# Sums of weight halves for the down product: from GpSimd subtracts during the up product to accumulating DRAM transfers, half of them in the front stages

## The chip, the cores and the metric

The kernel runs on one core of a Trainium2 chip (TensorE = PE, VectorE = DVE, ScalarE = ACT, GpSimd = POOL, and SyncE = SP, which here only issues DMAs). The metric is the device time of one execution, in microseconds (us); less is better. Times of three executions are given, and the trace of one of them.

## The reference

One layer of a bidirectional encoder block on 512 tokens of 1024 channels, all float32. What matters for the change is the last part, the channel mixer:

```python
h = rmsnorm(x, norm1_w); proj = h @ w_in          # p | q | k | v | z | gates | g_pool | g_dn
y_pool = (pooled p, linear map, scale) @ pool_out
o = gated_delta_rule(q, k, v) forward + backward   # 8 heads of 128, chunks of 64
y_dn = (rmsnorm(o) * silu(z)) @ dn_out
x = x + (sigmoid(g_pool) * y_pool + sigmoid(g_dn) * y_dn) @ w_o

h2 = rmsnorm(x, norm2_w)
u = dwconv_centered(h2 @ ffn_up, ffn_conv_w, ffn_conv_b)      # 1024 -> 2 * 2816, width 3
gate, val = split(u)
x = x + (silu(gate) * val) @ ffn_down                         # 2816 -> 1024
return rmsnorm(x, final_norm_w)
```

## The kernel before

**Products.** Each float32 operand is split into a rounded high part and a low part, and a product is three matmuls: high by high, high by low, low by high (`mm3`, L370). For the weights of a job, SP loads a block of 1024 x 128 (L387, 512 KB, `wr_...`), ACT casts it to the high part (L392, `wh_...`), and POOL subtracts the high part from the raw block in two halves (L396, `wl_...`). A matmul on the first half of the rows needs the first half of `wl`. The raw blocks live in a ring of three buffers, `wh` and `wl` in rings of two (`RINGS`, L243). A job of the up product is 24 matmuls of 512 columns.

**Stages.** First come the norm and the products with w_in (jobs named p, z, q, k, v, gp, gd), mixed with the pooled branch and the delta rule. The eight heads are taken in two groups of four. For each group the inverse of small triangular blocks is worked out on DVE (L897, L901), its rows are stored to DRAM scratch by SP (L923, `u_scr` and `e_scr`), and loaded again in another arrangement by `spread_unit` (L927): `nm` by SP, `ext` by ACT's queue (L944). `merge_unit` (L951) then begins with the matmuls `l1a` (L962), which read `nm` and `ext`. After that come dn_out, pool_out, w_o, the second norm, the up product (44 jobs, two for each of 22 blocks of 128 channels, followed by the convolution, SiLU and multiplication), the down product and the final norm.

**The down product** is done as seven products of half size in place of eight (`ORDER`, L1623: 1, 7, 5, 6, 3, 2, 4). The tokens are halved (`T_H`), the output columns are halved (`N_H`), and the 22 blocks of ffn_down's rows are two halves of `HK` = 11. Products 1, 2 and 3 take a quarter of ffn_down as their right operand; products 5, 6, 7 and 4 take the difference of two quarters. These differences are kept in DRAM, `t_scr[4, 11, 128, 512]`, index 0 for product 5, 1 for 6, 2 for 7 and 3 for 4. `right_operand` (L1820) says where a product reads, `down_weights` (L1830) loads two blocks of 128 x 512 at once (L1844, `wr_dn`), has ACT cast them (L1865) and POOL or DVE subtract (L1868). The left operands are combinations of the token halves, made by `combine` and `split_part` (L1634, L1641). When a product is complete, `done` (L1876) adds it to the residual `x2` by `dadd` (L1744).

**How the differences are made.** `t_unit` (L1649) is called for every second of the 22 channel blocks of the up product (L1714). It has SP load row block i of both halves of ffn_down into SBUF (L1656, two loads of 512 KB into `tp`), POOL do four subtracts (L1665), the third and fourth of which use the results of earlier ones, and SP store each difference of 256 KB to `t_scr` (L1667).

**What sets the order.** All steps are tasks with an engine, a cost, a key, buffers that they read and write, and for transfers a size. `Planner` (L38) schedules the list by these costs: an engine that is free takes the ready task with the lowest key, buffers of a ring are handed out in the order of the program, and a transfer is taken to occupy one shared channel at 280 KB per us and to land some us after its issue. The result is a fixed order per engine, and every engine works its own queue strictly in that order. A changed cost or task can so move instructions that have nothing to do with it. Keys begin with FEED (weights), EVICT (taking away results), CHAIN (delta rule) or a unit's number, in this order of rank. `after=` names buffers whose tasks must be done before a task may start.

Of the kernel before, what the change touches and what calls it, by code (L numbers as in the profile page):

```python
# [9 lines left out]
F32 = mybir.dt.float32  # L10
# [4 lines left out]
P = 128  # L15
# [180 lines left out]
def cp(n):  # L196
    return 0.17 + n * 0.0023
# [12 lines left out]
def hybrid_block(  # L210
# [1412 lines left out]
    ENDS = ((0, 1, 3), (0, 0, 2), (1, 1, 6), (1, 0, 4))  # L1623
    a_raw = [None, None]
# [24 lines left out]
    def t_unit(i, u):  # L1649

        b = {}

        def load(r):
            if "w" not in b:
                b["w"] = pools["fp"].tile([P, 2, D], F32, tag="tp", bufs=RINGS["tp"], name=f"tp_{i}")
            k = i + HK * r  # L1656
            sp.dma_start(b["w"][:, r, :], ffn_down[0][k * P : (k + 1) * P, :])

        w = lambda r, c: b["w"][:, r, N_H[c]]
        n = lambda r, c: f"tp:{i}#{r}{c}"  # L1660
        for r in range(2):
            L(512, lambda r=r: load(r), r=["pool:fp"], w=[n(r, 0), n(r, 1)], key=u)

        for j, o, x, y in ((0, (0, 0), (0, 1), (0, 0)), (2, (0, 1), (1, 1), (0, 1)), (1, (1, 1), (1, 1), (0, 0)), (3, (1, 0), (1, 0), (1, 1))):
            G(cp(512), lambda o=o, x=x, y=y: pool.tensor_tensor(out=w(*o), in0=w(*x), in1=w(*y), op=ALU.subtract),  # L1665
              r=[n(*x), n(*y)], w=[n(*o)], key=u)
            L(256, lambda j=j, o=o: sp.dma_start(t_scr[j, i], w(*o)), r=[n(*o)], w=[f"ts{j}#{i}"], key=u)  # L1667

    def conv3(box, pp, ci, b, j, u):
# [16 lines left out]
        for k in (0, 2):  # L1686
            V(0.78, lambda k=k: tap(k), r=[pp], w=[yn], key=EVICT + u)

    for c in range(NF):
# [20 lines left out]
        else:  # L1710
            i = c - HK
            combine(*blk(i, 1), blk(i, 1)[0], blk(c, 1)[0], [f"ar{c}#1"], ALU.add, u + 1)
            combine(*blk(i, 0), blk(i, 1)[0], blk(i, 0)[0], [f"ar{i}#1"], ALU.subtract, u + 2)
        if c % 2 == 0:  # L1714
            t_unit(c // 2, u + 60)
# [28 lines left out]
    def dadd(p, j, i, t, c0, c1):  # L1744
        dve.tensor_tensor(out=x2[t][:, c0:c1], in0=acc[accn(p, j, i)[1]][:, 0 : c1 - c0], in1=x2[t][:, c0:c1], op=ALU.add)
# [64 lines left out]
    def left_operand(p, key):  # L1810

        for i in range(0, HK, 2):
            n = min(2, HK - i)
            if p == 3:
                (x, xn), (y, yn) = blk(i + HK, 0, n), blk(i, 0, n)
                combine(y, yn, x, y, xn, ALU.subtract, key + 50 * i, n)
# [3 lines left out]
    def right_operand(p, k0, n):  # L1820
# [5 lines left out]
        return t_scr[j, k0 : k0 + n].rearrange("k p c -> p k c"), [f"ts{j}#{k}" for k in range(k0, k0 + n)]  # L1826
# [3 lines left out]
    def down_weights(p, kk, u):  # L1830
# [15 lines left out]
        L(n * 256, load, r=deps, w=[rn], key=FEED + u)  # L1846
# [119 lines left out]
```

## Time and profile before

| | |
|---|---|
| time, median of three executions | 892.42 us (890.75 to 892.56) |
| time of the profiled execution | 890.88 us |
| its span, first to last instruction | 889.2 us |
| PE busy | 874.7 us (98%) |
| POOL busy | 497.9 us (56%) |
| DVE busy, ACT busy | 549.0 us (62%), 461.0 us (52%) |
| granted PE clock, mean | 0.996 |
| DMA moved | 140.20 MB, mean 158 GB/s |
| HBM read, written | 114.08 MB, 25.20 MB |

In a row of the profile's groups stand line, engine, operation and tiles (output <- inputs, partitions x elements), a count, then busy us and mean ns of one, then the idle time of the engine ahead of these instructions and what ended most of it. A row of the list of waits gives the waiting instruction, what released it, us in all, count, and the longest. A row of the timeline gives start, duration, engine, line, operation, tiles and, in brackets, the idle time before. SPq and ACTq are the queues on which SP and ACT issue DMAs; the duration there is that of the issue. Rows of DMA issues end with the KB of one and the median us from issue to landing; rows of DMA queues hold packets, MB and the share of 16 engines' span. Matmuls overlap, so PE's starts tell more than its ends.

### The profile page before, as it was taken

What the parts mean: (1) busy time and instruction counts of PE and PEld (TensorE: products, weight loads), DVE (VectorE), ACT (ScalarE), POOL (GpSimd) and SP (SyncE); (2) the same over time, 40 slices, a digit from 0 to 9 for tenths busy, and PEclk for the clock granted to TensorE, in tenths of its full rate; (3) what the DMA queues carried; (4) which work ended last, traced back from release to release, by engine and by line L of the source; (5) the groups of instructions that cost most, each with busy time, mean ns of one, the idle gap of its engine ahead of it and who ended that gap; (6) DMA issues with size and microseconds to landing.
All of it is one profiled execution on the core that took longest, in us unless ns stands there. A gap on an engine that the chain in (4) does not pass through costs nothing.

```text
span 889.2 us, 14088 instructions
## 1 busy us (share of the span) xinstructions
PE 874.7 (98%) x5178; PEld 737.1 (83%) x5178; DVE 549.0 (62%) x980; ACT 461.0 (52%) x791; POOL 497.9 (56%) x447
## 2 busy tenths in 40 slices
PE   8999999999999999999999999999999999999996
PEld 7888888798878887988788888888888888888885
DVE  4757685357795976554434244656655554569995
ACT  6689533418868334335854334444443333456664
POOL 3444555125455553253668706778787764567663
PEclk9999999999999999999999999999999999999999
DMA  7365449324255376112898606567666753266553
GB/s 207 99 204 131 130 118 188 86 60 119 64 163 154 108 168 107 31 60 73 275 306 270 190 1 231 187 213 225 233 202 203 244 173 101 97 211 181 186 178 133
DMA packets 176265, 140.20 MB, mean 158 GB/s; under 512 B 32110, under 2 KB 143547, under 8 KB 176196
## 3 DMA queue, kind: packets, MB, share of 16 engines
q1 hardware_dynamic: 167300, 137.20, 51.1%
q10 hardware_dynamic: 8896, 2.10, 1.6%
q8 instruction: 41, 0.67, 0.3%
q14 instruction: 28, 0.23, 0.1%
HBM read 114.08 MB, written 25.20 MB: 157 GB/s over the span
## 4 chain that ended last, share of the span: by engine, by line
PE 92%; DVE 3%; ACT 2%; DMA 2%; issue 1%; SPq 0%; DVEq 0%; ACTq 0%
PE ps_up L372 9%; PE ps_up L371 9%; PE ps_up L373 9%; PE dn L373 3%; PE dn L371 3%; PE dn L372 3%; PE ps_k L371 2%; PE pw L1139 2%; PE o L1176 2%; PE ps_k L373 2%; PE ps_gp L371 2%; PE ps_k L372 2%; PE ps_wo L373 2%; PE ps_wo L372 2%; PE ps_wo L371 2%; PE ps_gp L372 2%
## 5 line engine op out<-in xcount | busy, mean ns | idle before, releaser
L396 POOL TENSOR_TENSOR wl_up<-wr_up,wh_up 128x512 fp32r<-128x512 f32 x88 | 115.2, 1330 | 50.1 <-ACT wh_up L392 47.9
L372 PE MATMUL ps_up<-h_lo,wh_up 128*128 128x512 f32 (+1 forms) x368 | 139.9, 380 | 0.3 <-DVE h_lo L541 0.3
L371 PE MATMUL ps_up<-h_hi,wh_up 128*128 128x512 f32 (+1 forms) x368 | 140.0, 380 | 0.0
L373 PE MATMUL ps_up<-h_hi,wl_up 128*128 128x512 f32 (+1 forms) x368 | 139.8, 380 | 0.0
L1680 DVE SCALAR_TENSOR_TENSOR c<-ps_up,fw,c 128x511 f32<-128x511 f32 x88 | 66.0, 750 | 99.3 <-ACT c L1674 97.5
L1665 POOL TENSOR_TENSOR tp<-tp 128x512 f32<-128x512 f32 x44 | 59.9, 1362 | 43.4 <-DMA tp<-in_ffn_down_dram 38.5
L1868 POOL TENSOR_TENSOR w_dn<-wr_dn,w_dn 128x512 fp32r<-128x512 f32 x44 | 65.6, 1504 | 29.0 <-ACT w_dn L1865 27.5
L372 PEld LDWEIGHTS ps_up<-h_lo,wh_up 128*128 128x128 f32 x368 | 69.1, 188 | 13.5 <-DVE h_lo L541 0.5
L371 PEld LDWEIGHTS ps_up<-h_hi,wh_up 128*128 128x128 f32 x368 | 69.1, 188 | 13.3
L373 PEld LDWEIGHTS ps_up<-h_hi,wl_up 128*128 128x128 f32 x368 | 69.1, 188 | 13.2
L392 ACT CAST wh_up<-wr_up 128x1024 fp32r<-128x1024 f32 x44 | 46.2, 1051 | 62.1 <-issue 22.3
L1865 ACT CAST w_dn<-wr_dn 128x512 fp32r<-128x512 f32 x69 | 42.4, 621 | 29.5 <-PE dn L373 21.1
L372 PE MATMUL dn<-w_dn,as 128*128 128x512 f32 x141 | 54.2, 385 | 0.0
L371 PE MATMUL dn<-w_dn,as 128*128 128x512 f32 x141 | 54.2, 384 | 0.0
L373 PE MATMUL dn<-w_dn,as 128*128 128x512 f32 x141 | 54.2, 384 | 0.0
L1634 DVE TENSOR_TENSOR as<-a,as 128x512 fp32r<-128x512 f32 (+1 forms) x41 | 41.8, 1044 | 0.1
L1630 ACT CAST as<-a 128x512 fp32r<-128x512 f32 (+1 forms) x41 | 21.5, 534 | 32.5 <-DVE a L1701 28.9
L396 POOL TENSOR_TENSOR wl_k<-wr_k,wh_k 128x512 fp32r<-128x512 f32 x16 | 20.3, 1288 | 31.6 <-ACT wh_k L392 22.4
L396 POOL TENSOR_TENSOR wl_v<-wr_v,wh_v 128x512 fp32r<-128x512 f32 x16 | 20.4, 1294 | 27.5 <-ACT wh_v L392 27.5
L1674 ACT ACTIVATE c<-ps_up,fw 128x512 f32<-128x512 f32 x44 | 33.9, 770 | 0.0
L396 POOL TENSOR_TENSOR wl_z<-wr_z,wh_z 128x512 fp32r<-128x512 f32 x16 | 20.3, 1292 | 23.5 <-ACT wh_z L392 19.9
L396 POOL TENSOR_TENSOR wl_gp<-wr_gp,wh_gp 128x512 fp32r<-128x512 f32 x16 | 21.5, 1360 | 19.6 <-ACT wh_gp L392 18.0
(361 smaller groups left out, 2435.8 us busy)
## 6 DMA issues: line engine op xcount, KB each, us to landing
wr_up<-in_ffn_up_dram SPq DMA_DIRECT2D x44, 512.0 KB, 3.9
tp<-in_ffn_down_dram SPq DMA_DIRECT2D x22, 512.0 KB, 5.3
t_scr<-tp SPq DMA_DIRECT2D x44, 256.0 KB, 2.5
wr_dn<-t_scr SPq DMA_DIRECT2D x20, 512.0 KB, 3.8
wr_dn<-in_ffn_down_dram SPq DMA_DIRECT2D x15, 512.0 KB, 3.6
x<-in_x_dram SPq DMA_DIRECT2D x8, 512.0 KB, 6.1
wr_k<-in_w_in_dram SPq DMA_DIRECT2D x8, 512.0 KB, 5.9
wr_z<-in_w_in_dram SPq DMA_DIRECT2D x8, 512.0 KB, 3.9
```

Source lines behind the costliest of these rows:

```text
L371: pe.matmul(ps, ahi, bhi, start=first, stop=False)
L372: pe.matmul(ps, ahi, blo, start=False, stop=False)
L373: pe.matmul(ps, alo, bhi, start=False, stop=last)
L392: act.copy(b["hi"], b["raw"])
L396: pool.tensor_tensor(out=b["lo"][:, sl], in0=b["raw"][:, sl], in1=f32(b["hi"][:, sl]), op=ALU.subtract)
L1630: act.copy(sets[p][:, i : i + n, 0, :], src())
L1634: dve.tensor_tensor(out=w[:, :, 1, :], in0=src(), in1=f32(w[:, :, 0, :]), op=ALU.subtract)
L1665: G(cp(512), lambda o=o, x=x, y=y: pool.tensor_tensor(out=w(*o), in0=w(*x), in1=w(*y), op=ALU.subtract), r=[n(*x), n(*y)], w=[n(*o)], key=u)
L1674: act.activation(b[j], box["ps"], AF.Identity, scale=fw[:, 1, ci : ci + 1], bias=fw[:, 3, ci : ci + 1])
L1680: dve.scalar_tensor_tensor(out=y[:, lo:hi], in0=box["ps"][:, lo + sh : hi + sh], scalar=fw[:, k, ci : ci + 1], in1=y[:, lo:hi], op0=ALU.mu ...
L1865: act.copy(b["w"][:, 0, :], raw["t"][:, j, :])
L1868: eng.tensor_tensor(out=b["w"][:, 1, :], in0=raw["t"][:, j, :], in1=f32(b["w"][:, 0, :]), op=ALU.subtract)
```

## The change

`t_unit` and its call are gone. In its place twelve calls of `right_sums`, each for one of the four scratch indices (in the order 0, 2, 1, 3) and four, four or three blocks of rows. Each call issues two DMAs on POOL's queue. The first copies a quarter's rows of ffn_down from DRAM to `t_scr` (for indices 1 and 3 it copies the sum that stands at index 0 or 1); the second adds another quarter's rows to that place in DRAM, by a transfer that accumulates. The planner is told 1.2 us of POOL's time for each and a landing after 12 us. Each first transfer is tied to the result of a job by its mark: six are front jobs (z3, z5, gd0, gd2, q4, q5), six are jobs of the up product (blocks 2, 5, 8, 11, 14, 17). So 24 transfers on POOL's queue take the place of 22 loads and 44 stores on SP's and 44 subtracts on POOL.

Sums take the place of differences. The signs are made good elsewhere: two combinations of the left operand change between add and subtract, and `dadd` adds or subtracts by the table `MINUS`, with `x2` as its first operand and PSUM as its second. The loads of right operands now also wait for the pool "fp" to be open, which the up product opens.

```diff
+    MINUS = ((0, 1, 1), (1, 1, 1), (1, 1, 7), (0, 1, 6), (1, 1, 6))
...
-    def t_unit(i, u):
...
-            L(512, lambda r=r: load(r), r=["pool:fp"], w=[n(r, 0), n(r, 1)], key=u)
...
-            G(cp(512), lambda o=o, x=x, y=y: pool.tensor_tensor(out=w(*o), in0=w(*x), in1=w(*y), op=ALU.subtract),
-              r=[n(*x), n(*y)], w=[n(*o)], key=u)
-            L(256, lambda j=j, o=o: sp.dma_start(t_scr[j, i], w(*o)), r=[n(*o)], w=[f"ts{j}#{i}"], key=u)
+    def right_sums(j, k0, n, key, after):
+
+        rows = lambda r: slice((k0 + HK * r) * P, (k0 + n + HK * r) * P)
+        block = lambda r, c: ffn_down[0][rows(r), N_H[c]]
+        flat_ = lambda j: t_scr[j, k0 : k0 + n].rearrange("k p c -> (k p) c")
+
+        first, second = {0: ((0, 0), (0, 1)), 1: (0, (1, 1)), 2: ((0, 1), (1, 1)), 3: (1, (1, 0))}[j]
+        kept = isinstance(first, int)
+        name = lambda j: [f"ts{j}#{k0}"]
+        move = lambda src, **kw: pool.dma_start(flat_(j), src, **kw)
+        add("pool", 1.2, lambda: move(flat_(first) if kept else block(*first)), name(first) if kept else [], name(j),
+            key, None, 256.0 * n, after=after, land=12.0)
+        add("pool", 1.2, lambda: move(block(*second), accum_op=ALU.add), [], name(j), key, None, 256.0 * n, land=12.0)
...
+    turn_ = [(j, k0, min(4, HK - k0)) for j in (0, 2, 1, 3) for k0 in (0, 4, 8)]
+    marks = ["pp:z3", "pp:z5", "pp:gd0", "pp:gd2", "pp:q4", "pp:q5"] + [f"pp:up{c}_0" for c in (2, 5, 8, 11, 14, 17)]
...
-        if c % 2 == 0:
-            t_unit(c // 2, u + 60)
+
+    for (j, k0, n), m in zip(turn_, marks):
+        right_sums(j, k0, n, EVICT, [m])
...
-    def dadd(p, j, i, t, c0, c1):
-        dve.tensor_tensor(out=x2[t][:, c0:c1], in0=acc[accn(p, j, i)[1]][:, 0 : c1 - c0], in1=x2[t][:, c0:c1], op=ALU.add)
+    def dadd(p, j, i, t, c0, c1, op):
+        dve.tensor_tensor(out=x2[t][:, c0:c1], in0=x2[t][:, c0:c1], in1=acc[accn(p, j, i)[1]][:, 0 : c1 - c0], op=op)
...
-        L(n * 256, load, r=deps, w=[rn], key=FEED + u)
+        L(n * 256, load, r=deps + ["pool:fp"], w=[rn], key=FEED + u)
```

The planner answers with another order on every engine. On POOL's queue in the front stages, between the jobs v1 and z5 (`wl` is the low part of a job's weights, `t_scr` the scratch of the sums, `bkd` and `qe` tiles of the delta rule), before:

```order
L396 TENSOR_TENSOR wl_v1_1105<-wr_v1_942,wh_v1_1104 128x512 [waits DMAHW0_49,PE_49,Activation_49]
L396 TENSOR_TENSOR wl_v1_1105<-wr_v1_942,wh_v1_1104 128x512
L814 TENSOR_TENSOR bkd_141<-bp_139,kdec_136 128x4x2 [waits DVE_49]
L396 TENSOR_TENSOR wl_z5_1176<-wr_z5_1012,wh_z5_1175 128x512 [waits DMAHW6_49,PE_49,Activation_49]
L396 TENSOR_TENSOR wl_z5_1176<-wr_z5_1012,wh_z5_1175 128x512
L1052 TENSOR_TENSOR qe_1_863<-qe_1_863,qT1_1203 128x384 [waits Activation_49]
```

and after:

```order
L1660 DMA t_scr_104<-in_ffn_down_dram 512x512
L396 TENSOR_TENSOR wl_v1_1106<-wr_v1_942,wh_v1_1105 128x512 [waits DMAHW0_49,PE_49,Activation_49]
L396 TENSOR_TENSOR wl_v1_1106<-wr_v1_942,wh_v1_1105 128x512
L814 TENSOR_TENSOR bkd_141<-bp_139,kdec_136 128x4x2 [waits DVE_49]
L396 TENSOR_TENSOR wl_z5_1177<-wr_z5_1012,wh_z5_1176 128x512 [waits DMAHW6_49,PE_49,Activation_49]
L396 TENSOR_TENSOR wl_z5_1177<-wr_z5_1012,wh_z5_1176 128x512
L1660 DMA t_scr_104<-in_ffn_down_dram 512x512 [waits DMASW0_49]
L1052 TENSOR_TENSOR qe_1_863<-qe_1_863,qT1_1204 128x384 [waits Activation_49]
```

The copy stands ahead of v1's low part, and the accumulate, which waits for the copy's landing, behind z5's: two jobs apart.

On SP's queue around the first group's scratch (`inv` and `rev` are the block inverses that are stored, `nm` the blocks loaded again for `l1a`, `wr_gd3` to `wr_k6` the weights of jobs), before:

```order
L387 DMA wr_gd2_1525<-in_w_in_dram 128x8x128
L923 DMA u_scr0_99<-inv_0_1561 16x4x1024
L923 DMA e_scr0_101<-inv_0_1561 16x4x1024
L387 DMA wr_gd3_1578<-in_w_in_dram 128x8x128
L923 DMA u_scr0_99<-rev_0_1583 16x4x1024
L923 DMA e_scr0_101<-rev_0_1583 16x4x1024
L1207 DMA gd_scr_106<-sgd_0_1607 128x512
L944 DMA nm_0_924<-u_scr0_99 32x32x32
L387 DMA wr_k4_1638<-in_w_in_dram 128x8x128
L944 DMA nm_0_924<-u_scr0_99 32x32x32 x3
L387 DMA wr_k5_1678<-in_w_in_dram 128x8x128
```

and after:

```order
L387 DMA wr_gd3_1562<-in_w_in_dram 128x8x128
L1207 DMA gd_scr_106<-sgd_0_1592 128x512
L387 DMA wr_k4_1628<-in_w_in_dram 128x8x128
L923 DMA u_scr0_99<-inv_0_1620 16x4x1024
L923 DMA e_scr0_101<-inv_0_1620 16x4x1024
L923 DMA u_scr0_99<-rev_0_1625 16x4x1024
L923 DMA e_scr0_101<-rev_0_1625 16x4x1024
L387 DMA wr_k5_1672<-in_w_in_dram 128x8x128
L1207 DMA gd_scr_106<-sgd_1_1688 128x512
L944 DMA nm_0_924<-u_scr0_99 32x32x32
L387 DMA wr_k6_1723<-in_w_in_dram 128x8x128
L944 DMA nm_0_924<-u_scr0_99 32x32x32 x3
```

The stores stood behind the loads of gd2 and gd3 and now stand behind that of k4; the last three loads of `nm` stood behind the load of k4 and now stand behind that of k6.

On PE, the matmuls just ahead of the first `l1a` (`ps_...` is the PSUM of a job, `pt_v3` a turning of v's channels into token order), before:

```order
L372 MATMUL ps_gd2_1684<-h_lo_153,wh_gd2_1644 128x512
L373 MATMUL ps_gd2_1684<-h_hi_152,wl_gd2_1645 128x512
L778 MATMUL pt_v3_1709<-ident_66,cv_v3_1654 128x128 x4
L371 MATMUL ps_gd2_1684<-h_hi_152,wh_gd2_1644 128x512
L372 MATMUL ps_gd2_1684<-h_lo_153,wh_gd2_1644 128x512
L373 MATMUL ps_gd2_1684<-h_hi_152,wl_gd2_1645 128x512
L962 MATMUL l1a_0_1724<-ext_0_391,nm_0_924 32x32 x16
```

and after:

```order
L371 MATMUL ps_k4_1772<-h_hi_152,wh_k4_1735 128x512
L372 MATMUL ps_k4_1772<-h_lo_153,wh_k4_1735 128x512
L373 MATMUL ps_k4_1772<-h_hi_152,wl_k4_1736 128x512
L371 MATMUL ps_k5_1807<-h_hi_152,wh_k5_1776 128x512
L372 MATMUL ps_k5_1807<-h_lo_153,wh_k5_1776 128x512
L373 MATMUL ps_k5_1807<-h_hi_152,wl_k5_1777 128x512
L962 MATMUL l1a_0_1814<-ext_0_391,nm_0_924 32x32 x16
```

The first `l1a` moved from behind row 660 to behind row 717 of PE's order: it comes after the rest of gd2, all of gd3 and k4 and the first three matmuls of k5.

19 lines of the change are left out of this document (5 added, 14 removed).

## The prediction

> **What bounds the kernel now.** I read the page's head first, then the list of PE's waits, then busy time in three stretches of 25 us, then single rows of the timeline.
>
> ```profile
> span 889.2 us, 14088 instructions
> PE 874.7 (98%) x5178; PEld 737.1 (83%) x5178; DVE 549.0 (62%) x980; ACT 461.0 (52%) x791; POOL 497.9 (56%) x447
> PE 92%; DVE 3%; ACT 2%; DMA 2%; issue 1%; SPq 0%; DVEq 0%; ACTq 0%
> ```
>
> PE is busy for 874.7 of 889.2 us, and the chain that ended last lies on PE for 92% of the span. All that any edit outside PE can win is the rest, 14.5 us. PE's list of waits (instruction <- releaser: idle us, count, longest) says what it is made of:
>
> ```profile
> PE pt_warm L574 <- POOL ident masks.py:199: 1.6, 1, 1.6
> PE l1a L962 <- ACT nm L1028: 1.4, 1, 1.4
> PE pt_v L778 <- ACT cv_v L763: 1.3, 1, 1.3
> PE pt_a L533 <- DVE xs L522: 0.9, 1, 0.9
> PE ps_po L371 <- DVE gpl L1395: 0.5, 1, 0.5
> PE ps_up L372 <- DVE h_lo L541: 0.3, 1, 0.3
> 881.35 0.28 PE L373 MATMUL dn<-wt_lo,as 128*128 128x256 f32 x1
> ```
>
> The first and the fourth belong to the program's head; the last matmul ends at 881.63, so 7.6 us are tail. The body holds 1.4 + 1.3 + 0.5 + 0.3 = 3.5 us of PE waits, 0.4% of the time. A gain can't be larger, unless PE's own work shrinks. The profiled execution took 890.88 us, 1.7 above its span and 1.5 below the median of 892.42; 0.2%, which is what a measurement here can tell from no change, is 1.8 us.
>
> The stretches (sum, then busy us of PE, PEld, DVE, ACT and POOL with counts, PE's granted clock, DMA share, GB/s) show the front of the up product, the down product and the end:
>
> ```profile
> 600.00:625.00 25.00, 25.00 (x112) 20.71 (x111) 14.54 (x18) 11.31 (x18) 19.75 (x16) 1.00 0.72 229
> 825.00:850.00 25.00, 25.00 (x112) 20.69 (x111) 25.00 (x30) 16.34 (x33) 17.95 (x13) 1.00 0.62 202
> ```
>
> PE has all 25 us in both, at a clock of 1.00, while the DMA engines are at 72% and POOL at 79%: neither of the things that the change relieves is what PE waits for.
>
> **The change part by part.** PE's instructions are the same in number (3771 rows in the order of either kernel), with the same shapes; only their order moves. Term: 0.
>
> Taken away are 22 loads of 512 KB, 44 subtracts on POOL and 44 stores of 256 KB:
>
> ```profile
> L1665 POOL TENSOR_TENSOR tp<-tp 128x512 f32<-128x512 f32 x44 | 59.9, 1362 | 43.4 <-DMA tp<-in_ffn_down_dram 38.5
> tp<-in_ffn_down_dram SPq DMA_DIRECT2D x22, 512.0 KB, 5.3
> t_scr<-tp SPq DMA_DIRECT2D x44, 256.0 KB, 2.5
> q1 hardware_dynamic: 167300, 137.20, 51.1%
> q10 hardware_dynamic: 8896, 2.10, 1.6%
> ```
>
> POOL loses 59.9 us of work. What that is worth is read where POOL feeds PE, in the up product:
>
> ```profile
> 738.22 1.05 ACT L392 CAST wh_up<-wr_up 128x1024 fp32r<-128x1024 f32 x1 [3.71 <-issue]
> 743.66 1.05 ACT L392 CAST wh_up<-wr_up 128x1024 fp32r<-128x1024 f32 x1 [1.42 <-PE ps_up L372]
> 728.47 2.54 POOL L396 TENSOR_TENSOR wl_up<-wr_up,wh_up 128x512 fp32r<-128x512 f32 x2 [2.90 <-ACT wh_up L392]
> 739.35 2.54 POOL L396 TENSOR_TENSOR wl_up<-wr_up,wh_up 128x512 fp32r<-128x512 f32 x2 [2.89 <-ACT wh_up L392]
> ```
>
> Jobs follow each other every 743.66 − 738.22 = 5.44 us. The first half of a job's low part is there at 739.35 + 2.54 / 2 = 740.6, and the next job's matmuls, which read it, begin at about 743.6: 3.0 us of slack, and POOL waits a further 2.9 us per job. So POOL is early by 5.9 us per job with the subtracts elsewhere, and taking them out wins nothing. Term: 0.
>
> Added are 24 transfers issued on POOL's queue: 12 copies (DRAM to DRAM, up to 1.05 MB) and 12 that accumulate onto them. What one issue costs POOL stands in no row. The nearest are issues on other queues:
>
> ```profile
> 604.47 0.33 SPq L1667 DMA_DIRECT2D t_scr<-tp  x1
> L944 ACTq DMA_DIRECT2D ext<-e_scr x8: 309/1018/2202, 145.0 to 331.0; - x8
> ```
>
> 0.33 to 2.2 us; I take 1.0, the median of the second row, since these issues are large as those are scattered. Behind the issue on POOL stands the low part of the next weights (wl), for which PE waits, and its 5.9 us cover all of the range. Term: 0; above 5.9 us each microsecond would count up to 24 times.
>
> Each accumulate waits on POOL until its copy has landed, and wl of the next job is queued behind that wait. The order puts at least two jobs between them, 2 × 5.44 = 10.9 us. A copy of 1 MB is not in the trace. Two bounds:
>
> ```profile
> wr_dn<-t_scr SPq DMA_DIRECT2D x20, 512.0 KB, 3.8
> wr_dn<-t_scr SPq DMA_DIRECT2D x4, 256.0 KB, 2.8
> m_scr<-gpl SPq DMA_DIRECT2D x8, 256.0 KB, 4.8
> ```
>
> From the first two, 1.0 us per further 256 KB: 3.8 + 2 × 1.0 = 5.8 us. From the third, 4 × 4.8 = 19.2 us. I take 5.8, since those rows are of the same scratch in pieces of the same length; then the copy is there 5 us before it is asked for. Term: 0 (range to the 30 us of the last rival).
>
> DMA load: 11.5 MB of loads and 11.5 MB of stores go, 11.5 MB of copies and 11.5 MB of accumulates come. By queue q1, engine time is 0.511 × 889.2 / 137.2 = 3.3 us of all 16 engines per MB; by q10, whose packets are small, 0.016 × 889.2 / 2.10 = 6.8. [...] That is spread over 500 us, and the up product's loads have room:
>
> ```profile
> 731.04 0.37 SPq L387 DMA_DIRECT2D wr_up<-in_ffn_up_dram  x1
> wr_up<-in_ffn_up_dram SPq DMA_DIRECT2D x44, 512.0 KB, 3.9
> ```
>
> With three raw buffers, a load goes out when the subtract that frees its buffer ends (728.47 + 2.54 = 731.0), and is cast three jobs on, at 743.66: 12.6 us for a load of 3.9, 8.7 us of slack. Term in the up product: 0. [...]
>
> **The place where it isn't hidden** is the merge of the first four heads, between 137 and 170 us. There the new order moves more than transfers:
>
> ```profile
> 137.09 0.57 SPq L923 DMA_DIRECT2D u_scr<-inv  x1
> 144.61 0.45 SPq L387 DMA_DIRECT2D wr_k<-in_w_in_dram  x1
> 145.11 4.21 SPq L944 DMA_DIRECT2D nm<-u_scr  x3
> nm<-u_scr SPq DMA_DIRECT2D x8, 128.0 KB, 7.1
> L962 PE MATMUL l1a<-ext,nm x256: 184/191/212, 156.4 to 352.5; 32*32 32x32 f32 x128
> 152.91 2.53 POOL L396 TENSOR_TENSOR wl_gd<-wr_gd,wh_gd 128x512 fp32r<-128x512 f32 x2 [2.92 <-ACT wh_gd L392]
> 155.47 0.38 SPq L387 DMA_DIRECT2D wr_k<-in_w_in_dram  x1
> 159.61 2.51 POOL L396 TENSOR_TENSOR wl_k<-wr_k,wh_k 128x512 fp32r<-128x512 f32 x2 [4.16 <-ACT wh_k L392]
> ```
>
> Before, the last block load ends its issue at 149.3, lands 7.1 later at 156.4, and l1a begins at 156.4. After, SP issues the last three block loads behind the load of k6, whose buffer comes free when wl of gd3 is done (152.91 + 2.53 = 155.4): issued until 155.5 + 0.4 + 4.2 = 160.1, landed at 167.2. PE reaches l1a 57 matmuls of 512 columns later than before; at 5.44 / 24 = 0.227 us each that is 12.9 us, 169.3. Slack 2.1 us without contention. But an accumulate of 0.79 MB is queued behind wl of gd3 (155.4) and a copy of 1.05 MB behind wl of k4 (162.1). Engine time asked for between 155.4 and 169.3, 13.9 us: two weight loads 1.05 MB × 3.3 = 3.5, three block loads 0.39 × 6.8 = 2.7, the accumulate 0.79 × 3.3 to 6.8 = 2.6 to 5.4, the copy 1.05 × 3.3 = 3.5; together 12.3 to 15.1. It fits, or is over by 1.2. I take +0.5, and keep 0 to 7 for the range.
>
> [...]
>
> The last additions swap their operands (PSUM as second, not first). The same shapes exist either way round, 186/347/405 ns with PSUM second and 197/357/417 with it first:
>
> ```profile
> L897 DVE TENSOR_TENSOR tmp<-n,un x60: 186/347/405, 106.6 to 317.4; 128x30 f32<-128x30 f32 x4, 128x58 f32<-128x58 f32 x4, 128x84 f32<-128x84 f32 x4, 128x108 f32<-128x108 f32 x4
> L901 DVE TENSOR_TENSOR un<-un,tmp x60: 197/357/417, 106.8 to 317.6; 128x30 f32<-128x30 f32 x4, 128x58 f32<-128x58 f32 x4, 128x84 f32<-128x84 f32 x4, 128x108 f32<-128x108 f32 x4
> ```
>
> Term: 0, to within 10 ns each, though DVE is full from 825 to 850. The body's four waits keep their 3.5 us for want of a reason.
>
> Sum: 890.88 + 0.5 = 891.4 for the profiled execution, 892.42 + 0.5 = 892.9 for the median.
>
> **The rivals.** *The waits go.* l1a comes 12.9 us later in the program, so its 1.4 us may vanish, and the re-planned front may also end the 1.3 us before pt_v: 892.42 − 2.7 = 889.7; with all of 3.5, 888.9. For it speaks that both are single waits behind chains on other engines that the new order lengthens or shortens at will; against it, that a chain moved is as likely to be late elsewhere: at the end of the second four heads the order now leaves fewer matmuls of cover than before. Also the change may then be worth nothing by itself: the gain would be the order's. Chance 0.24.
>
> *The accumulates hold the block loads.* If the transfers on POOL's queue get half of the engines while the block loads run, these take twice 7.1, so l1a is late by 7.1 − 2.1 = 5.0 us; if copy and accumulate go wholly ahead, 3.5 + 5.4 − 2.1 = 6.8. It decides once the block loads are delayed by more than 2.1 us; the time is 892.42 + 5.0 = 897.4 (894.2 to 899.2). For it: the engines are asked for 12.3 to 15.1 of 13.9 us. Against it: the copy goes out at 162.1, only 5 us before the loads are due. Chance 0.22.
>
> *POOL stands at the accumulate.* If a copy takes 19.2 us, it lands 19.2 − 10.9 = 8.3 after its accumulate's turn; 5.9 are covered, 2.4 × 12 = 29 us are not: 921. It decides from a landing of 16.8 us on. Only the m_scr row speaks for it. Chance 0.05.
>
> **How the numbers follow.** The forecast, 892.9 with its own range 890.6 to 894.2 (1.8 us either way of the median, for what can't be told apart), has 0.49. The range has to leave out no more than 0.2: it reaches down to 888.9, the first rival's end, and up to 898.5, most of the second's; outside remain the third and the tail of the second. Faster 0.24, same 0.49, slower 0.22 + 0.05 = 0.27.
>
> **What would show it.** Right: PE busy for 874 to 875 us, waits of PE in the body of 3 to 5 us, l1a released within 1 us of PE's reaching it, POOL busy for about 440 us plus its issues, and low parts in the up product as early as before. Wrong: a wait of PE at l1a of over 2 us whose chain goes back to the block loads (second rival); PE waiting for POOL's low parts just behind each accumulate (third); or PE waits in the body of under 1.7 us (first). If PE's busy time itself moves, the whole sum was set up wrongly.

## The result, and the profile after

The changed kernel takes 902.49 us (median of four executions, 900.84 to 905.55) against 892.49 us (median of four): a ratio of 1.0118, 95% interval 1.0083 to 1.0152. It is slower by 1.2%, above the range of 888.9 to 898.5. The profiled execution took 905.55 us, the slowest of the four, with a span of 903.8. Executions at a much lower mean clock than the others (two of the four in the first run with copies below, at 0.56 and 0.66) are left out of all ratios.

The page's head, and the stretches in which the up product and the down product run (columns as before):

```profile
span 903.8 us, 13921 instructions
PE 882.9 (98%) x5178; PEld 741.6 (82%) x5178; DVE 535.8 (59%) x980; ACT 466.1 (52%) x793; POOL 454.2 (50%) x427
PE 85%; DVE 6%; DMA 4%; ACT 3%; issue 1%; POOL 0%; ACTq 0%; SPq 0%; DVEq 0%; POOLq 0%
q0 software_dynamic: 7520, 23.07, 10.9%
```

```profile
600.00:625.00 25.00, 25.00 (x112) 20.71 (x111) 12.00 (x19) 11.53 (x16) 12.61 (x11) 1.00 0.54 160
825.00:850.00 25.00, 25.00 (x112) 20.71 (x111) 25.00 (x26) 13.76 (x25) 16.47 (x11) 1.00 0.61 195
```

In the up product POOL went from 19.75 to 12.61 busy us of 25 and the DMA share from 0.72 to 0.54, while PE had its 25.00 us and its 112 matmuls before and has them now. There the forecast holds: nothing was to be won. The first matmuls of the up product that show a gap in PE's row of starts stand at 541.28 before and at 555.59 after; from there to the end it is 347.9 us before and 348.2 after. All of the loss lies in the front stages.

PE's list of waits after:

```profile
PE l1a L962 <- DMA ext<-e_scr: 3.4, 2, 1.8
PE su L1154 <- ACT dt L733: 2.8, 1, 2.8
PE pkq L1062 <- ACT qT L765: 1.5, 1, 1.5
PE ps_p L371 <- ACT sgp L1204: 1.1, 1, 1.1
```

The waits of before at l1a (for nm) and pt_v are gone. In their place PE waits 3.4 us for `ext` (1.8 and 1.6 us, in the first merge, with four matmuls between), 2.8 us before `su`, and 1.5 and 1.1 us more. That is 8.8 us of named waits against 3.2 of before, and doesn't yet make 14.6 us of span. The rest is in PE's busy time, which rose from 874.7 to 882.9 us with the same 5178 matmuls. Four stretches, after and in the third experiment, which has the same order but no transfer in the front stages, show where (the last three columns are again PE's granted clock, the DMA share and GB/s):

```profile
160.00:174.70 14.70, 12.53 (x60) 9.95 (x58) 1.60 (x3) 4.70 (x6) 7.91 (x7) 1.00 1.19 247
174.70:181.50 6.80, 5.55 (x83) 3.99 (x83) 2.21 (x5) 1.62 (x5) 1.23 (x2) 0.50 1.15 288
240.00:256.60 16.60, 13.48 (x92) 11.74 (x91) 16.60 (x29) 12.67 (x21) 10.10 (x9) 1.00 0.59 140
256.60:260.00 3.40, 3.40 (x15) 3.18 (x15) 3.29 (x7) 0.57 (x1) 0.00 (x0) 0.50 0.86 216
```

```profile
174.70:181.50 6.80, 6.67 (x173) 4.92 (x172) 3.47 (x9) 3.26 (x11) 0.31 (x1) 1.00 0.32 80
256.60:260.00 3.40, 3.40 (x28) 3.25 (x28) 2.49 (x8) 1.81 (x4) 2.50 (x2) 1.00 0.30 113
```

Behind the first wait at l1a PE runs at a clock of 0.50 for 6.8 us, and behind the wait before `su` for 3.4 us. Matmuls of 512 columns start 0.43 us apart in the first of these stretches (177.53, 177.96, 178.39) and 0.23 us apart at a clock of 1.00 in the up product (606.04, 606.27, 606.49). Between 256.6 and 260.0 it does 15 matmuls where the other run, with other matmuls there, does 28. In these 10.2 us PE is busy for 5.55 + 3.40 = 8.95 us, of which half, 4.5 us, is lost to the clock; the rest is waiting that is counted already. Waits and clock together, 8.8 − 3.2 + 4.5 = 10.1 us. A further 2.7 us lie in the head, which no part of the change touches: the product for the gates, at 11.9 us before, comes at 14.6 here. In the profiled executions of the experiments it comes anywhere from 11.9 to 14.6 us, and at 14.6 in the first experiment, which is no slower than before, so these 2.7 us belong to the execution and not to the change. 12.8 of the 14.6 us are so named.

### The profile page after: what moved, and what is told of

It is laid out like the page before. It is cut to its first block, busy times and chain, and to the rows that moved or that the text cites. A ratio compares the mean times of both kernels' runs of the same rounds, so it can differ in the third digit from the quotient of the medians.

```text
span 903.8 us, 13921 instructions
## 1 busy us (share of the span) xinstructions
PE 882.9 (98%) x5178; PEld 741.6 (82%) x5178; DVE 535.8 (59%) x980; ACT 466.1 (52%) x793; POOL 454.2 (50%) x427
## 3 DMA queue, kind: packets, MB, share of 16 engines
q0 software_dynamic: 7520, 23.07, 10.9%
## 4 chain that ended last, share of the span: by engine, by line
PE 85%; DVE 6%; DMA 4%; ACT 3%; issue 1%; POOL 0%; ACTq 0%; SPq 0%; DVEq 0%; POOLq 0%
PE ps_up L372 9%; PE ps_up L373 9%; PE ps_up L371 9%; PE dn L373 3%; PE dn L371 3%; PE dn L372 3%; DVE dt L721 2%; PE ps_k L371 2%; PE ps_wo L373 2%; PE ps_wo L372 2%; PE ps_wo L371 2%; PE ps_z L373 2%; PE ps_z L372 2%; PE ps_z L371 2%; PE ps_do L373 2%; PE o L1176 2%
## 5 line engine op out<-in xcount | busy, mean ns | idle before, releaser
L396 POOL TENSOR_TENSOR wl_up<-wr_up,wh_up 128x512 fp32r<-128x512 f32 x88 | 111.9, 1292 | 146.5 <-ACT wh_up L392 146.5
L753 DVE SCALAR_TENSOR_TENSOR cv_k<-ps_k,cw,cv_k 128x510 f32<-128x510 f32 (+1 forms) x32 | 23.8, 748 | 23.6 <-ACT cv_k L747 22.8
L1636 DVE TENSOR_TENSOR as<-a,as 128x512 fp32r<-128x512 f32 (+1 forms) x41 | 36.4, 912 | 0.2
L721 DVE SCALAR_TENSOR_TENSOR dt<-dt,neg_g,mask 128x128 f32<-128x128 f32 x64 | 32.7, 576 | 3.8 <-ACT qe L730 3.8
L1702 ACT ACTIVATE c<-c 128x512 f32<-128x512 f32 x22 | 13.9, 633 | 33.8 <-DVE c L1676 33.8
```

What stands on the lines that cost most here:

```text
L396: pool.tensor_tensor(out=b["lo"][:, sl], in0=b["raw"][:, sl], in1=f32(b["hi"][:, sl]), op=ALU.subtract)
L721: dve.scalar_tensor_tensor(out=dts[h][:, d, t, :], in0=dts[h][:, d, t, :], scalar=neg_g[:, s_of(d, t), h, d : d + 1], in1=mask[:, d, :], o ...
L753: dve.scalar_tensor_tensor(out=y[:, lo:hi], in0=box["ps"][:, lo + sh : hi + sh], scalar=cw[:, k, ci : ci + 1], in1=y[:, lo:hi], op0=ALU.mu ...
L1636: dve.tensor_tensor(out=w[:, :, 1, :], in0=src(), in1=f32(w[:, :, 0, :]), op=ALU.subtract)
```

## The experiments

My first theory gave the loss two equal causes in the front stages: the transfers hold up the loads for the first l1a, and the new order puts decay arguments on DVE (`dt`, L721) beside POOL's subtracts. The rivals were contention alone, order alone, and a cost of the transfers and additions wherever they stand. Ratios are to runs of the kernel before on the same chip, with their 95% intervals. The edits are against the changed kernel and cut to the lines that matter; lists of marks are written short.

**All transfers late.** The marks are all jobs of the up product; the order ahead of it is that of before.

```diff
-    marks = ["pp:z3", "pp:z5", "pp:gd0", "pp:gd2", "pp:q4", "pp:q5"] + [f"pp:up{c}_0" for c in (2, 5, 8, 11, 14, 17)]
+    marks = [f"pp:up{c}_0" for c in (0, 2, 3, 5, 6, 8, 9, 11, 12, 14, 16, 18)]
```

> All 24 transfers are tied to jobs of the up product, none to the front stages; the order ahead of the up product is then that of before on every engine. Theory (two costs, both ahead of the up product: the transfers hold the loads for the first l1a back, and the new order puts decay arguments on DVE beside POOL's subtracts): both costs gone, 892 to 894 us, no PE wait over 1.5 us in the body that before doesn't have. Rival 'contention alone': the same, 892 to 894. Rival 'order alone': the same. Rival 'the loss is in the transfers, the sums or the additions to the residual themselves': 902 as in the changed kernel, since all of these are still there.

891.94 us, ratio 1.0005 (0.9994 to 1.0015). The transfers, the sums and the additions with swapped operands cost nothing by themselves; that rival falls. In this run, too, taking 44 subtracts and 66 DMAs away wins nothing.

**Front transfers, planned at no cost.** The planner is told neither POOL's time nor the size of the transfers, only their landing, and then gives every engine the order of before; six pairs run in the front stages.

```diff
-        add("pool", 1.2, lambda: move(flat_(first) ...
-            key, None, 256.0 * n, after=after, land=12.0)
-        add("pool", 1.2, lambda: move(block(*second), accum_op=ALU.add), [], name(j), key, None, 256.0 * n, land=12.0)
+        add("pool", 0.0, lambda: move(flat_(first) ...
+            key, None, 0.0, after=after, land=12.0)
+        add("pool", 0.0, lambda: move(block(*second), accum_op=ALU.add), [], name(j), key, None, 0.0, land=12.0)
...
-                    t.done = end
+                    t.done = end + (12.0 if t.land == 12.0 else 0.0)
```

> The planner is told that the transfers take nothing of POOL and of the shared channel (they still land after 12 us), so that every engine but POOL's added rows keeps the order of before in the front stages, while six copies and six accumulates run there. Theory (two costs of about 5 us each): 897 us (894 to 900), PE waits at the first l1a for nm or ext by 2 to 6 us and runs at a lower granted clock behind it, no wait of 2.8 us at su. Rival 'contention alone': 902. Rival 'order alone': 892 to 893, l1a as in before. Rival 'transfers or additions themselves': 902.

900.2 us, ratio 1.0096 (1.0076 to 1.0116). It is 9.0 us slower than before on the same chip (891.22) without any change of order, just above what my theory allowed. PE's waits that before doesn't have, or has shorter:

```profile
PE l1t L980 <- issue: 3.2, 2, 2.2
PE pt_v L778 <- ACT cv_v L763: 2.1, 1, 2.1
PE l1a L962 <- DMA ext<-e_scr: 1.6, 1, 1.6
```

The wait at `su` is gone, as expected; that for `ext` is shorter than the 2 to 6 us that I expected. Half clocks come here too, for 6.8 us from 171.8 on and for 3.4 us from 274.2 on. The row for l1t, a wait for nothing that the profile shows, is taken up below.

**The new order without the transfers.** All tasks stand in the plan as in the changed kernel, but the transfers are issued later, each third low part of the up product.

```diff
+        real[0].append(lambda: move(flat_(first) if kept else block(*first)))
+        real[1].append(lambda: move(block(*second), accum_op=ALU.add))
-        add("pool", 1.2, lambda: move(flat_(first) ...
+        add("pool", 1.2, lambda: None, ...
...
+        late = [f for i in range(0, 12, 2) for f in real[0][i : i + 2] + real[1][i : i + 2]]
+        seen = 0
         for t in ordered:
             t.fn()
+            if t.eng == "pool" and any(b.startswith("wlo:up") for b in t.uses):
+                if seen % 3 == 0 and late:
+                    late.pop(0)()
+                seen += 1
```

> Every engine has the order of the changed kernel, but all 24 transfers are issued later, behind low parts of the up product's weights; in the front stages none runs. Theory (two costs of about 5 us each): 897 us (894 to 900), first l1a without a wait over 1 us, but the wait of about 3 us at su near 250 us and 1.5 at pkq near 288 stay, with decay arguments (L721) of 1.4 us each beside POOL's subtracts. Rival 'contention alone': 892 to 893, the su wait gone. Rival 'order alone': 902. Rival 'transfers or additions themselves': 902.

892.56 us, ratio 1.0013 (1.0002 to 1.0024). My theory of two equal causes falls: the order alone costs about 1 us, the transfers in the front stages about 9. PE's list of waits in the body here:

```profile
PE pkq L1062 <- ACT qT L765: 1.5, 1, 1.5
PE ps_p L371 <- ACT sgp L1204: 1.1, 1, 1.1
PE su L1154 <- DVE rw L1143: 0.3, 1, 0.3
```

The waits at pkq and ps_p belong to the order; they about balance the l1a and pt_v waits that it removes. The `su` wait of 2.8 us that I had put down to the order is gone with the transfers, though the order of DVE and of POOL's other work is the same. POOL and DVE near it, first in the changed kernel, then here, show why:

```profile
248.65 1.09 POOL L1052 TENSOR_TENSOR qe<-qe,qT 128x384 f32<-128x384 f32 x1 [0.21 <-ACT qT L765]
249.67 1.05 POOL L1660 DMA_DIRECT2D t_scr<-in_ffn_down_dram  x1
250.34 1.41 POOL L1052 TENSOR_TENSOR qe<-qe,qT 128x384 f32<-128x384 f32 x1
251.59 2.61 POOL L396 TENSOR_TENSOR wl_q<-wr_q,wh_q 128x512 fp32r<-128x512 f32 x2
250.84 4.30 DVE L721 SCALAR_TENSOR_TENSOR dt<-dt,neg_g,mask 128x128 f32<-128x128 f32 x4
```

```profile
242.48 2.09 POOL L1052 TENSOR_TENSOR qe<-qe,qT 128x384 f32<-128x384 f32 x2 [0.22 <-PE pms L1251]
245.42 2.75 POOL L396 TENSOR_TENSOR wl_q<-wr_q,wh_q 128x512 fp32r<-128x512 f32 x2 [0.84 <-ACT wh_q L392]
244.66 1.13 DVE L721 SCALAR_TENSOR_TENSOR dt<-dt,neg_g,mask 128x128 f32<-128x128 f32 x4
```

Four decay arguments take 1.13 us when they fall into POOL's pause, and 4.30 when they start while POOL works: the first of them lasts 3.51 us, until POOL's chain of three operations is through. The accumulate's issue of 1.05 us between two `qe` closed that pause. `rw`, which `su` reads, stands behind the four on DVE and ends at 255.75; ACT's `dt`, which the list names, reads the same four and ends at 255.81. That the issue is what shifted POOL is read from the two traces; no run took that one issue away alone.

**Copies in place of accumulates**, first in the changed kernel's order, then in the order of before.

```diff
-        add("pool", 1.2, lambda: move(block(*second), accum_op=ALU.add), [], name(j), key, None, 256.0 * n, land=12.0)
+        add("pool", 1.2, lambda: move(block(*second)), [], name(j), key, None, 256.0 * n, land=12.0)
```

> The twelve accumulates are plain copies of the same rows (so the scratch holds one quarter of the weights in place of a sum). If an accumulate costs the DMA engines twice a copy: queue q0's share falls from 10.9% to about 7.3%, the wait at the first l1a falls by 1 to 3 us, 898 to 901 us. If an accumulate costs what a copy costs: share and time stay, 10.9% and 902 us.

899.07 and 901.14 us, ratio 1.0093 (1.0072 to 1.0114), inside the interval of the changed kernel. There is no trace of either of these two, so the queue is read from the second:

> The order of before and transfers in the front stages as in the run with the transfers planned at no cost, but the accumulates are plain copies of the same rows (so the scratch holds one quarter of the weights in place of a sum). If an accumulate holds the DMA engines longer than a copy: the gaps at l1t and the wait at l1a shrink by a half, 894 to 898; queue q0's share falls from 10.8% to about 7%. If it holds them no longer: 900, share as before.

898.3 us, ratio 1.0080 (1.0054 to 1.0106), against 1.0096 with accumulates. The page's row of the transfers' queue, with accumulates (second experiment) and with copies:

```profile
q0 software_dynamic: 7520, 23.07, 10.8%
```

```profile
q0 software_dynamic: 4704, 23.07, 6.9%
```

0.108 × 898.6 = 97.0 us of 16 engines against 0.069 × 893.4 = 61.6 for the same 23.07 MB. If half of the copies' 61.6 is the first transfers', the accumulates take 97.0 − 30.8 = 66.2 us for 11.5 MB, 5.7 us per MB against a copy's 2.7, 2.1 times as much, within the prediction's 3.3 to 6.8. In the profiled execution, the fastest of the four, the waits at l1t are gone and the one for `ext` stays:

```profile
PE l1a L962 <- DMA ext<-e_scr: 1.8, 1, 1.8
```

The time hardly follows: of the 9.0 us of the second experiment 6.9 are left. Neither "shrinks by a half" nor "stays" is right, and as far as four executions between 895.44 and 902.88 us can tell, most of the harm is done by traffic as such.

**Which pair does it.** With the transfers planned at no cost, single pairs are left in the front stages and the others go to the up product. First six pairs, placed where I took them to be clear of the first merge:

```diff
-    marks = ["pp:z3", "pp:z5", "pp:gd0", "pp:gd2", "pp:q4", "pp:q5"] + [f"pp:up{c}_0" for c in (2, 5, 8, 11, 14, 17)]
+    marks = ["pp:z0", "pp:z2", "pp:z4", "pp:k7", "pp:q5", "pp:q7"] + [f"pp:up{c}_0" for c in (2, 5, 8, 11, 14, 17)]
```

> The order of before on every engine, six copies and six accumulates in the front stages as in the run with the transfers planned at no cost, but three pairs are issued before the block rows are stored (some 75 to 125 us) and three after the first merge (some 190 to 300 us): none between 130 and 185 us. Theory (what costs time is where the transfers meet the first merge: its loads, and PE's own instructions, which it fetches in packets of 16 KB and uses up fastest there): 891 to 893.5 us, no half clock in the body. Rival (any megabyte moved in the front stages costs): about 900 as with all six there.

900.74 us, ratio 1.0099 (1.0080 to 1.0117): the number that the rival named. The waits say which part failed:

```profile
PE l1a L962 <- DMA ext<-e_scr: 3.6, 2, 2.0
PE pkq L1062 <- ACT qT L765: 2.7, 1, 2.7
```

This l1a is that of the second merge, at 345 us: the last pair's accumulate was issued at 332.11, just ahead of the second group's `ext` and `nm`. The first merge is as in before. Half clocks come with both, for 3.4 us from 300.0 on and for 6.8 us from 347.8 on. I had kept clear of one merge and hit the other; to tell this from a price by the megabyte, runs with fewer pairs. The first three alone:

```diff
-    marks = ["pp:z3", "pp:z5", "pp:gd0", "pp:gd2", "pp:q4", "pp:q5"] + [f"pp:up{c}_0" for c in (2, 5, 8, 11, 14, 17)]
+    marks = ["pp:z0", "pp:z2", "pp:z4"] + [f"pp:up{c}_0" for c in (5, 6, 8, 9, 11, 12, 14, 16, 18)]
```

> The order of before; three pairs in the front stages, all issued between some 66 and 120 us, nine in the up product. Theory (transfers cost only where they meet the loads of rows scattered through scratch, or PE's own instructions in a merge): 891 to 892.5 us, no PE wait in the body that before doesn't have. Rival (transfers in the front stages cost by the megabyte, 9 us for six pairs): about 895.

891.47 us, ratio 1.0003 (0.9993 to 1.0012): three pairs, issued between 54 and 113 us, cost nothing but a wait of 0.4 us for `ext`. There is no price by the megabyte. One pair alone, the fifth of the list, which the run clear of the first merge had at q5 as well:

```diff
-    marks = ["pp:z3", "pp:z5", "pp:gd0", "pp:gd2", "pp:q4", "pp:q5"] + [f"pp:up{c}_0" for c in (2, 5, 8, 11, 14, 17)]
+    marks = [f"pp:up{c}_0" for c in (0, 2, 3, 5)] + ["pp:q5"] + [f"pp:up{c}_0" for c in (8, 9, 11, 12, 14, 16, 18)]
```

> The order of before; only the pair tied to q5 (copy at about 270 us, accumulate at about 282) in the front stages. Theory: the load of rw from scratch (b_scr) for the second four heads lands 3 to 4 us later, ACT's copy of it is late, and PE waits at pkq for 2 to 3 us, with one window of half clock (1.7 us) behind: 894 to 896. Rival (the wait at pkq came from something else in that run): no wait there, 891 to 892.5.

896.22 us, ratio 1.0055 (1.0035 to 1.0075): a single pair costs 5.0 us, more than half of what all six do. The load of the block rows of the second four heads (`rw` and `n` from `b_scr`), and ACT's copy that waits for it, first in the run with all transfers late, then here:

```profile
rw<-b_scr SPq DMA_DIRECT2D x1, 256.0 KB, 3.7
n<-b_scr SPq DMA_DIRECT2D x1, 256.0 KB, 4.0
286.38 2.13 ACT L882 COPY n<-rw 64x1024 f32<-64x1024 f32 x1 [0.40 <-DMA rw<-b_scr]
```

```profile
rw<-b_scr SPq DMA_DIRECT2D x1, 256.0 KB, 5.2
n<-b_scr SPq DMA_DIRECT2D x1, 256.0 KB, 7.2
286.24 2.11 ACT L882 COPY n<-rw 64x1024 f32<-64x1024 f32 x1 [2.56 <-DMA rw<-b_scr]
PE pkq L1062 <- ACT qT L765: 2.2, 1, 2.2
```

The accumulate went out at 280.61, beside these loads; they land 1.5 and 3.2 us later, ACT's instructions in line behind the copy are late, and PE waits 2.2 us at pkq where before there was no wait. The profiled execution was the fastest of six, 892.6 us, and shows no half clock in the body; its mean clock is 0.997. The other five took 894.91 to 898.17 us at mean clocks of 0.993 to 0.995, and 0.003 of 893 us is 2.7 us. This cost explains the wait at pkq in that run, but can't be added to the changed kernel's or the second experiment's: there the pair at q5 is the sixth, of 0.79 MB. In the second experiment its accumulate goes out 0.9 us behind the issue of the load of `rw`, and not 0.4 us ahead of it as here, and PE's list has no wait at pkq.

The fourth pair alone, at gd2:

```diff
-    marks = ["pp:z3", "pp:z5", "pp:gd0", "pp:gd2", "pp:q4", "pp:q5"] + [f"pp:up{c}_0" for c in (2, 5, 8, 11, 14, 17)]
+    marks = [f"pp:up{c}_0" for c in (0, 2, 3)] + ["pp:gd2"] + [f"pp:up{c}_0" for c in (6, 8, 9, 11, 12, 14, 16, 18)]
```

> The order of before; only the pair tied to gd2 (1.05 MB copied, then accumulated) stands in the front stages. Its copy goes out at about 162 us, when the block rows have landed. Theory (PE waits for its own instructions): the first l1a waits 1.4 us as in before, no gap at instruction 1986, one of about 2 us at instruction 2242 (256 further on), and one or two windows of half clock behind it: 893.5 to 897. Rival (only the loads of the block rows are held up): 891 to 892.5, no gap.

891.88 us, ratio 1.0002 (0.9992 to 1.0013), no gap: my expectation fails, and by this run alone the rival stands. The packets below say why. The expectation also put before's wait of 1.4 us in the wrong place. It isn't at the first l1a but in the second merge; the row of before:

```profile
348.07 0.45 PE L962 MATMUL l1a<-ext,nm 32*32 32x32 f32 x32 [1.41 <-ACT nm L1028]
```

The third pair alone, at gd0:

```diff
-    marks = ["pp:z3", "pp:z5", "pp:gd0", "pp:gd2", "pp:q4", "pp:q5"] + [f"pp:up{c}_0" for c in (2, 5, 8, 11, 14, 17)]
+    marks = [f"pp:up{c}_0" for c in (0, 2)] + ["pp:gd0"] + [f"pp:up{c}_0" for c in (5, 6, 8, 9, 11, 12, 14, 16, 18)]
```

> The order of before; only the pair tied to gd0 (0.79 MB copied, then accumulated) stands in the front stages, the other eleven in the up product. Its copy goes out at about 145 us, beside the loads of the block rows, its accumulate at about 156, just ahead of the packets of PE instructions at 159 and 163 us. Theory: a wait of 1 to 2 us for ext or nm at the first l1a, one gap of about 1 us at l1t at the same place in PE's stream as before (instruction 1986 of the trace), one or two windows of half clock: 894 to 897. Rival (the gaps at l1t are chance or another engine's): no gap at 1986, 892 to 894.

894.68 us, ratio 1.0037 (1.0024 to 1.0049). PE's waits, as expected (but no half clock in the body):

```profile
PE l1a L962 <- DMA ext<-e_scr: 1.4, 1, 1.4
PE l1a L962 <- ACT nm L1028: 1.4, 1, 1.4
PE l1t L980 <- issue: 1.0, 1, 1.0
```

The second row is that of the second merge, as in before. The third is a wait for nothing that the profile shows. In the second experiment, with all six pairs, such waits at l1t last 1.1 and 2.2 us, and PE goes on at the 1986th and the 2242nd of its instructions in the trace, 256 apart; here at the 1986th again. The page counts 41 packets on an instruction queue with 0.67 MB together, 16 KB each; 41 times 256 is 10496, and the trace has 10483 instructions of PE. So I take a packet to hold 256 of them. The trace has the time of each:

```profile
q8 instruction: 41, 0.67, 0.3%
```

```
run                         instruction 1730   packet at, for us   instruction 1986
before                      158.7              159.0, 1.2          162.4
six pairs, order of before  160.4              163.1, 0.9          165.3
gd0 pair                    161.1              163.8, 1.0          166.0
gd2 pair                    159.1              159.7, 1.2          162.7
gd0 copy                    160.6              161.2, 1.2          164.3
gd0 accumulate              159.0              161.9, 1.0          164.4
```

In a merge, of many short matmuls, PE goes through 256 instructions in about 4 us. The packet with the next 256 comes 0.3 to 0.7 us after the boundary before in the three runs without an accumulate there, and 2.7 to 3.0 us after it beside the accumulate of the gd0 pair; PE then goes on 1.3 to 1.5 us behind the packet's end. The second wait of the second experiment, at 2242, has its packet 4.4 us after its boundary, beside that accumulate and the copy behind it. The gd2 pair's copy, issued at 162.46, came behind the packet of this boundary; of the next two packets the second began 1.4 us after its boundary (167.4), and PE had it just in time. With copies in place of accumulates the packet of 2242 comes 2.3 us after its boundary, and PE doesn't stop either. The last two runs take the gd0 pair apart.

Its second transfer gets a mark of its own; with the copy alone in its place the accumulate is tied to up5:

```diff
+    second_at = {(0, 8): ["pp:up5_0"]}
-        right_sums(j, k0, n, EVICT, [m])
+        right_sums(j, k0, n, EVICT, [m], second_at.get((j, k0), ()))
```

> As the run with the gd0 pair alone, but only its copy (at about 145 us) stays in the front stages; the accumulate goes to the up product. Theory: the copy holds the loads of ext and nm, the accumulate holds PE's instructions. So a wait of 1 to 1.5 us for ext at the first l1a, and no gap at instruction 1986: 892.5 to 894. Rival (one cause for both): the gap at 1986 stays.

With the accumulate alone the copy is tied to z3, well ahead, and the accumulate to gd1, which puts it behind gd3's low part:

```diff
-    marks = [f"pp:up{c}_0" for c in (0, 2)] + ["pp:gd0"] + [f"pp:up{c}_0" for c in (5, 6, 8, 9, 11, 12, 14, 16, 18)]
+    marks = [f"pp:up{c}_0" for c in (0, 2)] + ["pp:z3"] + [f"pp:up{c}_0" for c in (5, 6, 8, 9, 11, 12, 14, 16, 18)]
-    second_at = {(0, 8): ["pp:up5_0"]}
+    second_at = {(0, 8): ["pp:gd1"]}
```

> The other half of that pair: its copy goes out at about 107 us, only the accumulate stands at about 156 us. Theory: no wait for ext, a gap of about 1 us at instruction 1986 of PE, where the packet of instructions comes some 2 us late: 892 to 893.5. Rival (the gap is a result of the wait for ext): no gap, 891 to 892.

The copy alone: 894.96 us, ratio 1.0045 (1.0029 to 1.0060); the accumulate alone: 893.4 us, ratio 1.0023 (1.0011 to 1.0035). PE's waits with the copy, then with the accumulate:

```profile
PE l1a L962 <- DMA ext<-e_scr: 1.5, 1, 1.5
PE l1a L962 <- ACT nm L1028: 1.4, 1, 1.4
```

```profile
PE l1t L980 <- issue: 1.6, 1, 1.6
PE l1a L962 <- ACT nm L1028: 1.4, 1, 1.4
```

The two harms come apart as the theory has it: the copy at 145 us delays `ext` and not the packet, the accumulate at 156 us the packet and not `ext`. Only the size of the first is off: 3.7 us by the medians for a wait of 1.5. Its eleven executions run from 892.12 to 899.6 us, and the profiled one, with a span of 890.7, is near the fast end and has no half clock. The medians of the two halves, 3.7 and 2.2 us, also make more than the 3.3 us of the pair; that is not explained.

## Why the prediction was wrong

**What held.** In the up and the down product the terms came out at 0 together: the subtracts, the loads and stores, the issue on POOL there, the order of operands and the copies' landing cost nothing (ratio 1.0005 with all transfers there). No POOL stood at an accumulate there: of the first such pair in the changed kernel the copy goes out at 582.02, lands within 7 us, and the accumulate follows 10.9 us after it. The bound of 3.5 us on any gain held as well. Of the first rival half held: l1a's and pt_v's waits of before go with the new order, and two others of 1.5 and 1.1 us come for them, as the text said against it. But its reason for l1a was wrong. It took that wait to be at the first l1a, which now comes 12.9 us later; the wait stood in the second merge, at 348 us, so that it went there is luck. The 12.9 us themselves were right: PE reaches the first l1a at 172.0, with the head's 2.7 us taken off at 169.3, as forecast.

**The step that failed** is the term "+0.5" at the first merge, and with it the rest of the front stages. Three things were wrong in it.

First, it fixed the loads' landing and looked at half of them. The slack of 2.1 us was worked out for `nm` on SP's queue, with a landing of 7.1 us. PE waited last for `ext`, which ACT's queue loads, and whose issue the order had moved as well. In the third experiment, with the same order and no transfers, the last packets of `nm` and `ext` end at 166.8 and 169.1, ahead of PE at 172.0; here at 174.3 and 175.3. (Before, the last packets of `nm` end at 153.4, not at 156.4: the 7.1 us count from an issue's start, so that slack was sized too small. What failed is the 0.5 us allowed for the traffic.) The last load of `ext`, before and after, and the chain of waits after:

```profile
148.56 2.20 ACTq L944 DMA_DIRECT2D ext<-e_scr  x1
```

```profile
163.70 3.71 ACTq L944 DMA_DIRECT2D ext<-e_scr  x1
163.70 12.20 DMA ext<-e_scr
175.95 0.63 PE l1a L962 x22
```

The accumulate of 0.79 MB went out at 158.2, and its packets run from 161.7 to 167.1; the copy of 1.05 MB went out at 164.0, and its packets run from 168.1 to 173.1. The last load of `ext` took 12.2 us from the issue's start to its landing. The sum of engine time that "fits, or is over by 1.2" said nothing on that: 128 KB in packets of 128 bytes shared the engines with packets of 2 and 4 KB for most of that time. How the engines divide their time between the two isn't shown. The sum's 3.3 to 6.8 us per MB for an accumulate were the author's estimate from two other queues; no run shows that range for it, and the rows of q0 gave 5.7 by estimate. The second rival's picture (the loads take twice as long) was nearest, with 5.0 us at the same instruction against 3.4 measured.

Second, it took the front stages to have one such place. The experiments found four: the loads of `ext` and `nm` in both merges, the loads of `rw` and `n` from `b_scr`, and PE's own instructions in a merge. The changed kernel lost time at the first merge's loads; the other three are what other placings hit. The sentence "spread over 500 us" hid that a pair costs 0.02% or 0.55% of the time according to which of them it meets. And the 5.9 us that cover POOL's issue were read in the up product and carried to the front stages, where, by the two traces above, 1.05 us of issue before four decay arguments cost 2.8 us at `su`.

Third, "PE's instructions are the same in number, with the same shapes; term: 0" left out that their speed isn't fixed. With waits of 3.4 us (in two, the clock drops between them) and 2.8 us came 6.8 and 3.4 us at a clock of 0.50, which adds 4.5 us to 6.2 us of waiting. The second rival's 897.4 with the first stretch's share of it, 5.55 / 2 = 2.8 us, is 900.2, still without `su`. A rival that prices a wait by its own length alone leaves these 4.5 us out.

That the chances gave "slower" 0.27 goes back to this: the places where transfers do harm were not looked for one by one.

## What to carry to other kernels

Before moving bulk transfers to an earlier stage, list what in that stage goes through DRAM in small pieces with something waiting right behind it, PE's instruction packets where matmuls are short included, and keep the transfers out of those stretches; in the others they may cost nothing (three early pairs here: ratio 1.0003). Allow for more than the length of a wait of PE: here waits of 1.6 us (the gd0 accumulate) to 3.4 us (the changed kernel, in two) had a half clock of 3.4 or 6.8 us behind them, by estimate up to 1.7 or 3.4 us more, while waits of 1.5 us (the gd0 copy) and 2.2 us (the pair at q5) had none in the profiled executions. Relieving what nothing waited for, POOL and the DMA engines in the up product, won nothing here (ratio 1.0005 with all transfers there).

## What the runs showed of the hardware

**PE waits for its own code.** The page has 41 packets on the instruction queue, 0.67 MB, so 16 KB each, and by the count above 256 instructions. In the first merge they come one boundary ahead; in the runs of the order of before, packets that came 2.7 to 4.4 us after their boundary stopped PE for 1.0 to 2.2 us at a place where the profile names no releaser. PE's lists of waits show such a stop only there, in the three runs of that order that have the gd0 accumulate in the first merge (1.1 and 2.2, 1.0, and 1.6 us).

**DVE's decay arguments are slow beside POOL.** An L721 operation, both of whose tensors lie in SBUF, lasts 0.34 us alone, 1.37 beside POOL's subtracts, and once 3.51, until three of POOL's operations in a row were through. What holds it isn't shown.

**The half clock falls on a grid of 3.413 us in these traces.** In the changed kernel's it begins at 174.69 and 256.61 us, 24 times 3.413 us apart, and lasts 6.83 and 3.41 us; in the second experiment's at 7.99, 171.83 and 274.23 us, 48 and 30 times 3.413 us apart. Taking the traces of this case on that grid between 20 and 870 us (without the first run with copies), PE was busy for 0.7 to 1.9 of the 3.4 us just ahead of each of the eight drops (1.25 and 0.72 us in the changed kernel); it was busy for 1.9 us or more in every other window at full clock but one, with 1.7 (the pair at q5). Waits of 1.5 us (the gd0 copy) and 2.2 us (the pair at q5) left the clock alone in the profiled executions; one of 1.6 us (the gd0 accumulate) was followed by 3.4 us of half clock, from 166.3 us on. So the length of a wait alone doesn't tell these cases apart; how it falls on the windows may, as an inference from these few. It may also be why the executions of these kernels lie further apart (892.12 to 899.6 us with the gd0 copy) than those of before (889.67 to 893.66); no trace of one at the long end is there to show it.
